# Projecting the queries of all eight heads in one pass of 512 columns, in place of two passes of 256

## The chip, the cores and the metric

One NeuronCore of a Trainium2 chip. The metric is the device time of one execution in microseconds. The profile's engines are PE (TensorE, the matmuls), DVE (VectorE), ACT (ScalarE), POOL (GpSimd) and SP (SyncE, which issues most DMAs).

## The reference

Two trunk layers over 512 latent tokens and 256 context tokens of width 1024. In each layer one input projection feeds three mixers: centred pooling, gated linear attention (GLA) and softmax attention with eight query heads and two key/value heads of 64 channels. The part of the softmax attention:

```python
u = (rmsnorm(x, g_mix) * (1 + sc1) + sh1) @ w_in        # and the same for the context, uc
p, gq, gk, gv, gg, rf, rb, aq, ak, av = split_in(u)     # aq: 512 columns, ak, av: 128 each
q = rmsnorm(q.reshape(B, N, 8, 64), g_q)                # per head, with a scale of 1/8 in the scores
ql = axial_rope(ql, rows, cols)                         # latent queries and keys only
o = softmax(q @ k.T / 8) @ v                            # latent queries see context and latent keys
mix = concat(pool_mixer(p), gla_output(o_gl, gg), o) @ w_out
x = x + ga1 * mix
x = x + ga2 * squared_relu_mlp(rmsnorm(x, g_mlp) * (1 + sc2) + sh2)
```

## The kernel before

Everything is fp32. For the large products each operand is split into a high and a low part in a rounded fp32 format (`whi`, `wlo` of the weights, `hTh`, `hTl` of the transposed activations), and each product is made of three matmuls: high by high, low by high, high by low. `tm_matmul` writes 128 tokens by some columns of weights: over 8 slices of the contraction it issues 24 matmuls for one token tile. Six token tiles are live in layer 0 (four latent, two context) and four in layer 1. `wcols` loads weights in pieces of 512 KB (`raw`, on SP's queue), ScalarE rounds them to `whi`, VectorE or GpSimd subtracts to `wlo`.

`q_proj(cb)` projects the queries of four heads: 256 columns for each live tile, one PSUM tile `tm` each, and ScalarE copies it to `Uq[cb][g]`, which holds up to three token tiles. After each group of three tiles (or the last tile) come `head_norm` (ScalarE squares into `sq`, VectorE sums it to `ssa`, makes the inverse root `rsa` in tiny steps, and multiplies, L874) and the rotary product `rope_mult`: four multiplications on GpSimd from `Uq` into `sq` (L863), one on VectorE in place (L865), which must wait until GpSimd has read `Uq`, and a sum (L866). The context queries in a group are multiplied by a gain instead. `q_proj(0)` goes over all tiles, then `q_proj(1)`.

The same stage holds GLA for two pairs of heads. For a pair, eight levels (s = 0, 1, 2, 4, ... 64) each make 48 or 24 small matmuls (`att`, L764) from `QQ` and `KK` (below s = 32 from a copy `kc` of `KK` that ScalarE makes). Between two levels VectorE multiplies `QQ` and `KK` in place by decays (L721, four per level), so the next level's matmuls wait for it. After the last level the chunks of `KK` are transposed (`kbt`), copied (`kbT`) and multiplied (`inc`). The output of a pair is `o`, then `ss`, `rg` and `ogl`, which ScalarE, VectorE, GpSimd and ScalarE (`mixh`) finish in turn.

What runs when is written as generators: `g` the GLA of both pairs, `a` the projections (`a_thread`: gates, keys and values, queries, and the pooling projections `p_proj`, whose PSUM tile is `fm`), `m` the modulation (`pm`, `pt`, `brow`), `t` the attention (`kT`, `qT`, `sc`, ...). A string of letters per layer deals out their steps; the first `t` runs what is left of `a`. A scheduler then fixes one order for each engine, and each engine runs its own in order:

```python
ths = {"g": gla_thread(), "a": at_, "m": mods, "t": att_}
for ch in STEPS[l]:
    if ch == "t":
        run(at_)
    next(ths[ch], None)
```

Of the kernel before, what the change touches and what calls it, by code (L numbers as in the profile page):

```python
# [14 lines left out]
ALU = mybir.AluOpType  # L15
# [6 lines left out]
KT = 8  # L22
# [12 lines left out]
def hybrid_kernel(ctx, tc, x, c, cx, c_ctx, w_mod, b_mod, g_mix, w_in, w_pool, s_pool, w_gate, b_gate,  # L35
# [20 lines left out]
    def slot(s, dt=F32, w=NT):  # L56
        return sp.tile([128, w], dt, tag="S", name=nm(s))
# [105 lines left out]
    def wcols(w, c0, n, ksplit, *more, sl=False):  # L163

        parts = []
        step = KT // ksplit
        for s in range(ksplit):
            parts.append(wload(*(w[s * step * 128:(s + 1) * step * 128, a:a + m].rearrange("(k p) n -> p k n", p=128)
                                 for a, m in ((c0, n),) + more), sl=sl))
        return lambda k: (parts[k // step][0][:, k % step], parts[k // step][1][:, k % step])  # L170
# [156 lines left out]
    def tm_matmul(ps, t, wk, hT, nk, c0=0, n=None, k0=0, k1=None):  # L327

        for k in range(k0, k1 or nk):
            wh, wl = wk(k)  # L330
            hh, hl = hT[k]
            sl = slice(t * 128, (t + 1) * 128)
            for i, (a, b) in enumerate(((hh, wh), (hl, wh), (hh, wl))):
                bb = b if n is None else b[:, c0:c0 + n]
                T.matmul(ps, a[:, sl], bb, start=(k == 0 and i == 0), stop=(k == nk - 1 and i == 2))  # L335
# [83 lines left out]
    for l in range(2):  # L419
# [163 lines left out]
        def gslot(s, tag, dt=F32, bufs=1, w=NT):  # L583
            return gp.tile([128, w], dt, tag=tag, name=nm(s), bufs=bufs)
# [52 lines left out]
        def gate_proj(pr):  # L637

            wk = wcols(W, C_GG + pr * 128, 128, 1)
            ps = psA("fm")  # L640
            fm_matmul(ps, wk, hT, KT, True, both)
            g_ = slot("gate")
            gx, tmp = g_[:, 0:N_], gslot("sg", "gt", bufs=GT)[:, 0:N_]
            A.activation(gx, ps[:, 0:N_], AF.Copy)
            gate[pr] = g_
            yield
            V.tensor_scalar(tmp, gx, -87.0, None, ALU.max)
            A.activation(tmp, tmp, AF.Exp, scale=-1.0)
            A.activation(tmp, tmp, AF.Ln, bias=one)
            A.activation(tmp, tmp, AF.Exp, scale=-1.0)  # L650
            V.scalar_tensor_tensor(gx, tmp, gglaT, gx, ALU.mult, ALU.mult)
# [205 lines left out]
        def rope_mult(v, tab, tmp, nt, nh):  # L857

            for half in range(2):
                for z in range(2):  # L860
                    d0 = half * 32 + z * 16
                    s0 = half * 32 + (1 - z) * 16
                    G.tensor_tensor(tmp[:, :, :, d0:d0 + 16], v[:, :, :, s0:s0 + 16],  # L863
                                    tab[:, 1, :, d0:d0 + 16].unsqueeze(2).to_broadcast([128, nt, nh, 16]), ALU.mult)
            V.tensor_tensor(v, v, tab[:, 0].unsqueeze(2).to_broadcast([128, nt, nh, 64]), ALU.mult)  # L865
            V.tensor_tensor(v, v, tmp, ALU.add)  # L866

        def head_norm(v, sq, nh, post=None):

            A.activation(sq, v, AF.Square)  # L870
            ss = mp.tile([128, nh], F32, tag="ssa", name=nm("ssa"))
            V.tensor_reduce(ss, sq, AX.X, ALU.add)
            r = rstd_of(ss, 64, "rsa", post)
            V.tensor_tensor(v, v, r.unsqueeze(2).to_broadcast([128, nh, 64]), ALU.mult)  # L874

        def k_proj():
            wk = wcols(W, C_AQ + 512, 256, 2)
            UK = slot("UK")
            UKt.append(UK)
            UV = slot("UV")  # L880
            UVt.append(UV)
            for t in alltiles:
                ps = psB("tm")
                tm_matmul(ps[:, 0:256], t, wk, hT, KT)
                A.activation(UK[:, t * 128:(t + 1) * 128], ps[:, 0:128], AF.Copy)
                A.activation(UV[:, t * 128:(t + 1) * 128], ps[:, 128:256], AF.Copy)  # L886
                yield
            sq = gslot("sq", "gt", bufs=GT)
            head_norm(UK.rearrange("p (m e) -> p m e", e=64), sq.rearrange("p (m e) -> p m e", e=64), 12)
            yield  # L890
            rope_mult(UK[:, 0:NL].rearrange("p (t h e) -> p t h e", h=2, e=64), rk,
                      sq[:, 0:NL].rearrange("p (t h e) -> p t h e", h=2, e=64), 4, 2)
            kc = UK[:, NL:NT].rearrange("p (m e) -> p m e", e=64)
            V.tensor_tensor(kc, kc, gr[:, 1].unsqueeze(1).to_broadcast([128, 4, 64]), ALU.mult)
            yield

        def q_proj(cb):
            wk = wcols(W, C_AQ + cb * 256, 256, 2)
            for t in live:
                g = t // 3  # L900
                if t % 3 == 0:
                    Uq[cb][g] = slot("Uq")
                uq = Uq[cb][g]
                ps = psB("tm")
                tm_matmul(ps[:, 0:256], t, wk, hT, KT)
                A.activation(uq[:, (t % 3) * 256:(t % 3) * 256 + 256], ps[:, 0:256], AF.Copy)
                yield
                if t % 3 == 2 or t == live[-1]:
                    nt = t % 3 + 1
                    sq = gslot("sq", "gt", bufs=GT)[:, 0:nt * 256]  # L910
                    uv_ = uq[:, 0:nt * 256]
                    head_norm(uv_.rearrange("p (m e) -> p m e", e=64), sq.rearrange("p (m e) -> p m e", e=64), nt * 4, 0.125)
                    yield
                    nr = nt if g == 0 else 1
                    u4 = uv_.rearrange("p (t h e) -> p t h e", h=4, e=64)
                    s4 = sq.rearrange("p (t h e) -> p t h e", h=4, e=64)
                    rope_mult(u4[:, 0:nr], rq[:, :, 3 * g:3 * g + nr], s4[:, 0:nr], nr, 4)
                    if nr < nt:
                        qc = uq[:, nr * 256:nt * 256].rearrange("p (m e) -> p m e", e=64)
                        V.tensor_tensor(qc, qc, gr[:, 0].unsqueeze(1).to_broadcast([128, (nt - nr) * 4, 64]), ALU.mult)  # L920
                    yield

        def p_proj(bp_):
            wk = wcols(W, bp_ * 128, 128, 1)
            ps = psA("fm")
            fm_matmul(ps, wk, hT, KT, True, both)
            m_ = slot("pm")
            A.activation(m_[:, 0:N_], ps[:, 0:N_], AF.Copy)
            pmt[bp_] = m_
            yield  # L930

        def a_thread():
            for qk in range(2):
                qk_proj(1, qk)
                yield
            for th in (gate_proj(0), gate_proj(1), k_proj(), q_proj(0), q_proj(1), p_proj(0), p_proj(1)):
                yield from th


# [384 lines left out]
```

## Time and profile before

| | us |
|---|---|
| median of three runs | 1680.46 (1678.68 to 1682.53) |
| the profiled execution | 1677.11 |
| its span | 1675.3 |
| TensorE busy | 1599.7 (95%) |
| VectorE busy | 910.4 (54%) |
| ScalarE busy | 642.4 (38%) |
| GpSimd busy | 414.2 (25%) |

The span runs from the first to the last instruction on the core; 1.8 us of the execution lie around it. A table of stretches gives, for each window of time, its length and the busy time of PE, weight loads (PEld), DVE, ACT and POOL, then the clock that TensorE was granted (1.00 is full speed), the busy share of the DMA engines and GB/s. In the group rows the last parts are busy time and mean ns of one, then the engine's idle time just before and what ended it. In the chain, each row is start, length and what the end of the program hung on at that time.

### The profile page before, as it was taken

The numbers are of one execution on the slowest core, as the hardware profiler recorded it, in microseconds if no ns is written. First come the engines' busy times: TensorE is split into PE (matmuls) and PEld (weight loads), VectorE is DVE, ScalarE is ACT, GpSimd is POOL, SyncE is SP. The second block draws the span as 40 slices with busy tenths as digits, with TensorE's granted clock in tenths as the row PEclk, the third lists the DMA queues.
The fourth block names the chain that finished last, engine by engine and source line by source line (L and its number), as shares of the span: only waits on it lengthen the run. The fifth ranks groups of instructions, "written<-read, shape, count | busy, mean of one in ns | idle before, by whom it ended". The sixth has DMA issues, their size and how long they took to land.

```text
span 1675.3 us, 27451 instructions
## 1 busy us (share of the span) xinstructions
PE 1599.7 (95%) x11403; PEld 1301.5 (78%) x11403; DVE 910.4 (54%) x1306; ACT 642.4 (38%) x1098; POOL 414.2 (25%) x484
## 2 busy tenths in 40 slices
PE   7999979999999999999999999897999999999997
PEld 4888856668888888888888889785667888888885
DVE  4437665743673654636546563586753645455544
ACT  5544445661531312213213244556662523223332
POOL 1121311212303032130321462241201122222225
PEclk9999989999999999999999999998999999999998
DMA  9445400222340421514424332100123313333331
GB/s 318 139 131 172 154 2 1 103 88 64 101 139 26 144 95 57 176 59 161 144 71 170 112 106 74 39 2 2 52 83 94 109 55 101 101 101 101 101 101 51
DMA packets 136636, 163.31 MB, mean 97 GB/s; under 512 B 9908, under 2 KB 108608, under 8 KB 136512
## 3 DMA queue, kind: packets, MB, share of 16 engines
q1 hardware_dynamic: 130176, 148.41, 27.7%
q10 hardware_dynamic: 5824, 13.12, 2.1%
q8 instruction: 89, 1.46, 0.4%
q14 instruction: 35, 0.29, 0.1%
q0 software_dynamic: 512, 0.03, 0.0%
HBM read 157.31 MB, written 4.23 MB: 96 GB/s over the span
## 4 chain that ended last, share of the span: by engine, by line
PE 85%; DVE 5%; ACT 4%; issue 2%; POOL 2%; DMA 2%; ACTq 0%; SPq 0%; POOLq 0%; DVEq 0%
PE dn L335 25%; PE up L316 19%; PE tm L335 7%; PE op L335 6%; PE up L318 5%; PE fm L316 4%; PE av L1055 3%; PE pT L1046 3%; PE up L325 2%; PE fm L318 1%; PE sc L1028 1%; PE att L764 1%; PE sc L1029 1%; PE pm L190 1%; DVE nmx L1031 1%
## 5 line engine op out<-in xcount | busy, mean ns | idle before, releaser
L159 ACT ACTIVATE whi<-raw 128x1024 fp32r<-128x1024 f32 (+2 forms) x182 | 185.0, 1031 | 568.6 <-PE dn L335 292.7
L1179 POOL TENSOR_TENSOR X<-X,rtmp 128x512 f32<-128x512 f32 x158 | 216.8, 1375 | 636.2 <-DVE rtmp L1178 636.0
L78 DVE TENSOR_TENSOR wlo<-raw,whi 128x1024 fp32r<-128x1024 f32 (+2 forms) x182 | 224.9, 1245 | 219.7 <-ACT whi L159 215.4
L1178 DVE TENSOR_TENSOR rtmp<-dn,ga 128x512 f32<-128x512 f32 x160 | 109.4, 688 | 213.4 <-PE dn L335 210.5
L335 PE MATMUL dn<-whi,ah 128*128 128x512 f32 x480 | 187.3, 390 | 0.0
L335 PE MATMUL dn<-whi,al 128*128 128x512 f32 x480 | 187.2, 390 | 0.0
L335 PE MATMUL dn<-wlo,ah 128*128 128x512 f32 x480 | 186.3, 390 | 0.0
L316 PE MATMUL up<-h2h,whi 128*128 128x512 f32 x464 | 182.5, 393 | 1.5 <-ACT relu L1221 1.5
L316 PE MATMUL up<-h2h,wlo 128*128 128x512 f32 x464 | 183.1, 395 | 0.0
L316 PE MATMUL up<-h2l,whi 128*128 128x512 f32 x464 | 182.8, 394 | 0.0
L335 PEld LDWEIGHTS dn<-whi,ah 128*128 128x128 f32 x480 | 90.1, 188 | 20.2 <-issue 0.8
L316 PEld LDWEIGHTS up<-h2h,whi 128*128 128x128 f32 x464 | 87.1, 188 | 23.4 <-ACT relu L1221 1.7
L335 PEld LDWEIGHTS dn<-whi,al 128*128 128x128 f32 x480 | 90.1, 188 | 19.5
L335 PEld LDWEIGHTS dn<-wlo,ah 128*128 128x128 f32 x480 | 90.1, 188 | 19.0
L316 PEld LDWEIGHTS up<-h2l,whi 128*128 128x128 f32 x464 | 87.1, 188 | 21.7 <-issue 2.5
L335 PE MATMUL tm<-whi,hTh 128*128 128x256 f32 (+1 forms) x352 | 102.2, 292 | 1.0 <-ACT UV L886 1.0
L316 PEld LDWEIGHTS up<-h2h,wlo 128*128 128x128 f32 x464 | 87.1, 188 | 19.5
L335 PE MATMUL tm<-whi,hTl 128*128 128x256 f32 (+1 forms) x352 | 100.7, 287 | 0.0
L335 PE MATMUL tm<-wlo,hTh 128*128 128x256 f32 (+1 forms) x352 | 100.3, 288 | 0.0
L335 PE MATMUL dn<-whi,a 128*128 128x512 f32 x320 | 99.9, 395 | 0.4 <-DVE rtmp L1178 0.4
L228 DVE SCALAR_TENSOR_TENSOR macc<-rawm,sstat,macc 128x1024 f32<-128x1024 f32 x56 | 75.6, 1370 | 7.9 <-DMA rawm<-in_w_mod_dram 7.4
L1031 DVE TENSOR_REDUCE nmx<-sc 128x1 f32<-128x768 f32 x64 | 60.6, 955 | 28.1 <-PE sc L1029 27.6
(295 smaller groups left out, 3329.9 us busy)
## 6 DMA issues: line engine op xcount, KB each, us to landing
rawm<-in_w_mod_dram SPq DMA_DIRECT2D x80, 512.0 KB, 5.6
raw<-in_w_up_dram SPq DMA_DIRECT2D x64, 512.0 KB, 4.2
raw<-in_w_down_dram SPq DMA_DIRECT2D x64, 512.0 KB, 4.4
raw<-in_w_in_dram SPq DMA_DIRECT2D x26, 512.0 KB, 4.0
rawm<-in_w_mod_dram SPq DMA_DIRECT2D x32, 256.0 KB, 5.4
raw<-in_w_out_dram SPq DMA_DIRECT2D x16, 512.0 KB, 4.4
raw<-in_w_in_dram SPq DMA_DIRECT2D x12, 256.0 KB, 3.0
ga<-gaD ACTq DMA_DIRECT2D x6, 512.0 KB
```

What stands on the lines that cost most here:

```text
L78: V.tensor_tensor(lo, full, hi.bitcast(F32), ALU.subtract)
L159: A.activation(hi, raw, AF.Copy)
L228: V.scalar_tensor_tensor(acc[s], raw, c_, acc[s], ALU.mult, ALU.add)
L316: T.matmul(ps[:, 0:NL], a, b[:, 0:NL], start=st, stop=sp_)
L318: T.matmul(ps[:, NL:NT], a, b[:, NL:NT], start=st, stop=sp_)
L325: T.matmul(ps[:, cs], a, b[:, cs], start=(k == 0 and i == 0), stop=(k == nk - 1 and i == 2))
L335: T.matmul(ps, a[:, sl], bb, start=(k == 0 and i == 0), stop=(k == nk - 1 and i == 2))
L1031: V.tensor_reduce(nmx[:, i:i + 1], sv, AX.X, ALU.max, negate=True)
L1046: T.transpose(pt_[:, i * 128:(i + 1) * 128], p_[:, ki * 128:(ki + 1) * 128], ident)
L1055: T.matmul(av_[64 * hh:64 * hh + 64, 0:256], vst, pe[:, hh * 256:hh * 256 + 256], start=(ki == 0), stop=(ki == len(kts) - 1))
L1178: V.tensor_tensor(tmp, ps, ga[0 if t < 4 else 1][:, sl], ALU.mult)
L1179: (V if b == NB - 1 and not both and t == 3 else G).tensor_tensor(X[t][:, sl], X[t][:, sl], tmp, ALU.add)
```

## The change

`q_proj` takes all 512 columns at once. For each live tile there are 24 matmuls of 512 columns in place of twice 24 of 256, in one PSUM tile, from which ScalarE copies two halves. The weights come in four pieces of 512 KB, of which all must be there for each tile, in place of two and two. The head norms and rotary products of the two halves follow each other after each group of tiles. In all 480 matmuls of 256 columns (and 480 weight loads) become 240 of 512; the counts of the other engines' instructions hardly change. A projection step now holds a tile of 512 columns, and the projection thread has 14 steps left of it where it had 20 in layer 0 and 12 where it had 16 in layer 1; the string that deals out the steps is the same.

```diff
-        def q_proj(cb):
-            wk = wcols(W, C_AQ + cb * 256, 256, 2)
+        def q_proj():
+            wk = wcols(W, C_AQ, 512, 4)
             for t in live:
                 g = t // 3
                 if t % 3 == 0:
-                    Uq[cb][g] = slot("Uq")
-                uq = Uq[cb][g]
+                    for cb in range(2):
+                        Uq[cb][g] = slot("Uq")
                 ps = psB("tm")
-                tm_matmul(ps[:, 0:256], t, wk, hT, KT)
-                A.activation(uq[:, (t % 3) * 256:(t % 3) * 256 + 256], ps[:, 0:256], AF.Copy)
+                tm_matmul(ps, t, wk, hT, KT)
+                for cb in range(2):
+                    A.activation(Uq[cb][g][:, (t % 3) * 256:(t % 3) * 256 + 256], ps[:, cb * 256:(cb + 1) * 256], AF.Copy)
                 yield
                 if t % 3 == 2 or t == live[-1]:
                     nt = t % 3 + 1
-                    sq = gslot("sq", "gt", bufs=GT)[:, 0:nt * 256]
...
+                    for cb in range(2):
+                        uq = Uq[cb][g]
+                        sq = gslot("sq", "gt", bufs=GT)[:, 0:nt * 256]
...
-            for th in (gate_proj(0), gate_proj(1), k_proj(), q_proj(0), q_proj(1), p_proj(0), p_proj(1)):
+            for th in (gate_proj(0), gate_proj(1), k_proj(), q_proj(), p_proj(0), p_proj(1)):
```

The orders differ in layer 0 from the first query tile to the first score, and in the same part of layer 1. In the rows below a name's number tells one buffer from another: `QQ_1163` and `KK_773` belong to GLA's first pair of heads, `QQ_2463` (before `QQ_2452`) and `KK_992` to its second, `Uq_1632`, `Uq_1644` and `Uq_1645` hold queries of the first three tiles, `UK` keys.

TensorE's queue in layer 0 at the level s = 64 of the first pair (`att` of 64x64), before; the `tm` rows are matmuls of one 256-column tile:

```order
L335 MATMUL tm_2041<-whi_1628,hTl_136 128x256
L764 MATMUL att_1957<-QQ_1163,KK_773 64x64 x2
L335 MATMUL tm_2041<-wlo_1629,hTh_135 128x256
L335 MATMUL tm_2041<-whi_1628,hTh_137 128x256
L764 MATMUL att_1957<-QQ_1163,KK_773 64x64 x22
L202 MATMUL pt_2030<-ident,brow_2024 128x128 x4
L335 MATMUL tm_2041<-whi_1628,hTl_138 128x256
```

and after, where the row on top ends a 512-column tile:

```order
L335 MATMUL tm_2026<-wlo_1641,hTh_141 128x512
L764 MATMUL att_1885<-QQ_1163,KK_773 32x32 x48
L190 MATMUL pm_995<-rawm_1999,sstat 32x512 x2
L190 MATMUL pm_995<-rawm_2003,sstat 32x512 x2
L764 MATMUL att_1960<-QQ_1163,KK_773 64x64 x24
L202 MATMUL pt_2013<-ident,brow_2007 128x128 x4
L695 MATMUL kbt_2054<-ident,KK_773 128x128 x6
L695 MATMUL kbt_2142<-ident,KK_773 128x128 x6
L190 MATMUL pm_2023<-rawm_2106,sstat 32x512 x2
```

The levels s = 32 and s = 64 and the transposes `kbt` now stand together, with only modulation matmuls between them; before, a good part of a tile stood ahead of each.

VectorE's queue at the same place, before (the rows on `tree` multiply `QQ` and `KK` for the next level, 12x32 behind s = 32 and 6x64 behind s = 64):

```order
L874 TENSOR_TENSOR Uq_1632<-Uq_1632,rsa_1845 128x768
L721 TENSOR_TENSOR QQ_1163<-QQ_1163,tree_1065 128x12x32
L721 TENSOR_TENSOR KK_773<-KK_773,tree_1065 128x12x32
L721 TENSOR_TENSOR QQ_1163<-QQ_1163,tree_1155 128x12x32
L721 TENSOR_TENSOR KK_773<-KK_773,tree_1155 128x12x32
L865 TENSOR_TENSOR Uq_1632<-Uq_1632,rq_756 128x768
L199 TENSOR_TENSOR brow_2024<-pm_995,brow_2024 128x512
L866 TENSOR_TENSOR Uq_1632<-Uq_1632,sq_1841 128x768
L78 TENSOR_TENSOR wlo_2157<-raw_2154,whi_2156 128x1024
L721 TENSOR_TENSOR QQ_1163<-QQ_1163,tree_1065 128x6x64
L721 TENSOR_TENSOR KK_773<-KK_773,tree_1065 128x6x64
L721 TENSOR_TENSOR QQ_1163<-QQ_1163,tree_1155 128x6x64
```

and after:

```order
L874 TENSOR_TENSOR Uq_1644<-Uq_1644,rsa_1861 128x768
L874 TENSOR_TENSOR Uq_1645<-Uq_1645,rsa_1950 128x768
L865 TENSOR_TENSOR Uq_1644<-Uq_1644,rq_756 128x768
L721 TENSOR_TENSOR QQ_1163<-QQ_1163,tree_1065 128x12x32
L721 TENSOR_TENSOR KK_773<-KK_773,tree_1065 128x12x32
L721 TENSOR_TENSOR QQ_1163<-QQ_1163,tree_1155 128x12x32
L721 TENSOR_TENSOR KK_773<-KK_773,tree_1155 128x12x32
L866 TENSOR_TENSOR Uq_1644<-Uq_1644,sq_1857 128x768
L199 TENSOR_TENSOR brow_2007<-pm_995,brow_2007 128x512
L865 TENSOR_TENSOR Uq_1645<-Uq_1645,rq_756 128x768
L721 TENSOR_TENSOR QQ_1163<-QQ_1163,tree_1065 128x6x64
L721 TENSOR_TENSOR KK_773<-KK_773,tree_1065 128x6x64
```

The norms of both halves and the first rotary product now stand ahead of the first four multiplications, and the second rotary product ahead of the last four.

TensorE's queue in layer 0 at `rg` of the first pair's output, before; `tm_2463` is the last query tile, and behind its 24 matmuls come the rest of the level `att_2570` and both `p_proj`:

```order
L190 MATMUL pm_2040<-rawm_2455,sstat 32x512 x2
L190 MATMUL pm_2040<-rawm_2459,sstat 32x512 x2
L764 MATMUL att_2503<-gq_935,KK_992 32x32 x48
L190 MATMUL pm_2040<-rawm_2555,sstat 32x512 x2
L190 MATMUL pm_2040<-rawm_2559,sstat 32x512 x2
L764 MATMUL att_2570<-QQ_2452,KK_992 32x32 x11
L828 MATMUL rg_2429<-ident,rsg_2420 64x128 x8
L828 MATMUL rg_2440<-ident,rsg_2420 64x128 x4
L335 MATMUL tm_2463<-whi_2150,hTh_127 128x256
L335 MATMUL tm_2463<-whi_2150,hTl_128 128x256
```

and after, where the row on top is the last of the second `p_proj`:

```order
L318 MATMUL fm_2367<-hTh_141,wlo_2364 128x256
L828 MATMUL rg_2440<-ident,rsg_2431 64x128 x8
L828 MATMUL rg_2451<-ident,rsg_2431 64x128 x4
L764 MATMUL att_2474<-gq_935,KK_992 32x32 x48
L764 MATMUL att_2534<-QQ_2463,KK_992 32x32 x48
L202 MATMUL pt_2668<-ident,brow_2662 128x128 x4
L1086 MATMUL qT_2697<-ident,Uq_1644 128x128 x3
L1086 MATMUL qT_2697<-ident,Uq_2024 128x128
L1086 MATMUL qT_2698<-ident,Uq_2024 128x128 x2
L1086 MATMUL qT_2998<-ident,Uq_1644 128x128 x3
L1086 MATMUL qT_2998<-ident,Uq_2024 128x128
L764 MATMUL att_2597<-QQ_2463,kc_2598 32x32 x48
```

Both `p_proj` and the last query tiles have moved ahead of `rg`, and the first levels of the second pair, the key and query transposes and the first scores follow it directly.

More of the change, by code (lines that the diff above doesn't have):

```diff
@@ L909, in q_proj @@
                     nt = t % 3 + 1
-                    sq = gslot("sq", "gt", bufs=GT)[:, 0:nt * 256]
[L911 to L921, printed above, removed]
+                    for cb in range(2):
+                        uq = Uq[cb][g]
+                        sq = gslot("sq", "gt", bufs=GT)[:, 0:nt * 256]
+                        uv_ = uq[:, 0:nt * 256]
+                        head_norm(uv_.rearrange("p (m e) -> p m e", e=64), sq.rearrange("p (m e) -> p m e", e=64), nt * 4,
+                                  0.125)
+                        yield
+                        nr = nt if g == 0 else 1
+                        u4 = uv_.rearrange("p (t h e) -> p t h e", h=4, e=64)
+                        s4 = sq.rearrange("p (t h e) -> p t h e", h=4, e=64)
+                        rope_mult(u4[:, 0:nr], rq[:, :, 3 * g:3 * g + nr], s4[:, 0:nr], nr, 4)
+                        if nr < nt:
+                            qc = uq[:, nr * 256:nt * 256].rearrange("p (m e) -> p m e", e=64)
+                            V.tensor_tensor(qc, qc, gr[:, 0].unsqueeze(1).to_broadcast([128, (nt - nr) * 4, 64]), ALU.mult)
+                        yield
         def p_proj(bp_):
```

## The prediction

> **What bounds the kernel now.** I read the page first, for the engine that sets the end, then a table of stretches, for where that engine idles, then groups, waits and the chain inside the stretches that the change touches.
>
> ```profile
> span 1675.3 us, 27451 instructions
> PE 1599.7 (95%) x11403; PEld 1301.5 (78%) x11403; DVE 910.4 (54%) x1306; ACT 642.4 (38%) x1098; POOL 414.2 (25%) x484
> PE 85%; DVE 5%; ACT 4%; issue 2%; POOL 2%; DMA 2%; ACTq 0%; SPq 0%; POOLq 0%; DVEq 0%
> raw<-in_w_in_dram SPq DMA_DIRECT2D x26, 512.0 KB, 4.0
> ```
>
> TensorE is busy 95% of the span and is 85% of the chain that ends last. So two things can move the time: the length of the matmul stream, and the few stretches where TensorE waits. The stretches around the query projection, first of layer 0, then (from 1134) of layer 1; the granted clock stands after POOL's busy time:
>
> ```profile
> 130.00:140.00 10.00, 9.58 (x254) 9.18 (x253) 5.83 (x15) 4.10 (x10) 0.00 (x0) 1.00 0.66 225
> 140.00:150.00 10.00, 8.79 (x156) 6.57 (x156) 7.53 (x16) 2.59 (x5) 2.71 (x4) 1.00 0.35 118
> 150.00:160.00 10.00, 10.00 (x255) 8.51 (x254) 8.19 (x17) 7.35 (x22) 2.56 (x4) 1.00 0.22 57
> 160.00:170.00 10.00, 9.91 (x148) 7.47 (x147) 8.53 (x22) 5.52 (x11) 2.49 (x6) 1.00 0.85 274
> 220.00:230.00 10.00, 6.86 (x227) 4.95 (x225) 7.64 (x17) 5.70 (x10) 2.80 (x5) 0.98 0.02 5
> 230.00:240.00 10.00, 7.34 (x194) 5.71 (x194) 8.83 (x16) 3.65 (x7) 2.71 (x8) 0.51 0.01 2
> 250.00:260.00 10.00, 10.00 (x112) 7.06 (x112) 5.45 (x10) 6.25 (x13) 0.00 (x0) 0.82 0.01 2
> 1134.00:1140.00 6.00, 1.84 (x71) 1.40 (x70) 1.59 (x3) 3.13 (x6) 2.68 (x3) 0.80 0.01 3
> ```
>
> From 150 to 170 TensorE is full although VectorE works 8.2 and 8.5 of 10 us: the 256-column query tiles stand between the gated-linear-attention (GLA) levels and hide the chains that those levels need. Where that cover ends (220 to 240, 1134 to 1140) TensorE starves and the granted clock drops to about a half: 0.51 follows a stretch with 3.14 us of idle time.
>
> **The matmuls themselves.** 480 matmuls of 256 columns become 240 of 512. Their prices in the chain:
>
> ```profile
> 129.96 3.60 PE tm L335 x30
> 175.22 5.95 PE tm L335 x48
> 168.98 3.07 PE tm L335 x24
> 513.27 32.66 PE dn L335 x144
> ```
>
> One of 256 columns costs 5.95/48 = 124 ns, or at its best 3.60/30 = 120.0 ns; one of 512 costs 32.66/144 = 226.8 ns. A pair of 256 gives 248 or 240, so a 512 saves 21 or 13 ns, and 240 of them 5.0 or 3.1 us. I take 4.0 and keep both ends. The Trainium skill, "TensorE: Matmul & The Clock Gate", section "Wait — 56ns, not 53.3ns?", says that warm matmuls start N/2.4 GHz plus about 2.5 ns apart; by it a pair saves only 2.5 ns, an estimate of 0.6 us in all, which would put my time some 3.4 us higher. The rows show five to eight times that per pair, and the measured rows decide.
>
> The weights are the same bytes in four pieces of 512 KB, as before, but all four must now be there for the first tile: two pieces come earlier. They are asked for on SP's queue behind modulation loads, and a piece lands in 4.0 us. In the rows of 130 to 150, where the tiles stand, the DMA engines are at 0.66 and 0.35, so there is room, and the last piece is first used some three quarters into the first tile. I cost this at nothing; if that cover were gone, one landing of 4.0 us would stand in the first tile.
>
> **The order: levels of the first pair of heads.** The program's steps are dealt out by a fixed string; a projection step is now twice as long, there are six fewer of them in layer 0 and four fewer in layer 1, and so all later steps meet other work. Behind the third tile TensorE runs one level's matmuls, one whole tile, the level s = 32, and then nothing but the level s = 64, a modulation transpose (pt) and the chunk transposes (kbt). Before, most of a tile stood ahead of each. On VectorE the normalisations (L874) of both halves and the first rotary product (L865), which waits for POOL, stand ahead of the four multiplications (L721) that the level s = 64 needs; the second rotary product stands ahead of the four that kbt needs. Prices, from 140 to 170 (VectorE) and 140 to 235 us:
>
> ```profile
> L874 DVE TENSOR_TENSOR Uq<-Uq,rsa 128x768 f32<-128x768 f32 x2 | 1.9, 954 | 0.0
> L872 DVE TENSOR_REDUCE ssa<-sq 128x12 f32<-128x768 f32 x2 | 1.9, 953 | 1.6 <-ACT sq L870 1.6
> L784 DVE COPY_PREDICATED dg<-mask,att 128x192 f32<-128x192 int32 x6 | 1.9, 365 | 0.0
> L865 DVE TENSOR_TENSOR Uq<-Uq,rq 128x768 f32<-128x768 f32 x1 | 0.9, 946 | 0.0
> L199 DVE TENSOR_TENSOR brow<-pm,brow 128x512 f32<-128x512 f32 x1 | 0.7, 677 | 0.0
> L260 DVE SCALAR_TENSOR_TENSOR rsa<-rsa,ssa 128x12 f32<-128x12 f32 x2 | 0.3, 172 | 0.2
> L863 POOL TENSOR_TENSOR sq<-Uq,rq 128x192 f32<-128x192 f32 x8 | 4.8, 633 | 14.2 <-DVE Uq L874 14.2
> L906 ACT ACTIVATE Uq<-tm 128x256 f32<-128x256 f32 x11 | 4.2, 384 | 22.9 <-PE tm L335 22.8
> L870 ACT ACTIVATE sq<-Uq 128x768 f32<-128x768 f32 x4 | 3.4, 840 | 0.2
> 162.94 0.47 DVE QQ L721
> 152.39 3.18 PE tm L335 x25
> 156.06 0.91 PE att L764 x62
> 164.96 0.85 PE kbt L695 x6
> 165.81 1.85 PE pm L190 x16
> ```
>
> Count from the end of the third tile. ScalarE: two evictions (0.77) and two squares (1.68), first square done at 1.6, second at 2.4. VectorE: two reductions to 3.5; two multiplications and two predicated copies of the level (0.5 and 0.37 each) to 5.3; ten tiny steps of some 0.2 (0.17 and the gap) to 7.3; the two L874 to 8.3 and 9.2. POOL's first set of four (2.5) ends at 10.8, L865 at 11.8, four L721 at 13.7. TensorE: level 1.0, modulation 0.9, a tile of 24 x 227 ns = 5.4, level 1.0, modulation 0.5 or so: free at 8.9. It waits 4.8 us. Then the level s = 64 (0.5) ends at 14.2; pt waits for the other half of the rotation (0.95) and L199 (0.68) until 15.3, 1.1 us; kbt waits for the second L865 and two L721 until 17.2, with pt at 0.6 another 1.3 us. Together 7 us where TensorE before waited 0.09 (160 to 170). Of the 1.6 us that it waited from 130 to 150 some may go, since fewer and larger steps run there. I take +5.5; bounds +2 (POOL's set hidden in another order of arrivals) and +8.
>
> The half clock comes with such a wait. In the row of 250 to 260 TensorE is full at 0.82, so 1.8 us are lost while it has work; the second loss (0.51) fell where it mostly waited. I take +1.7; bounds 0 and 3.5. The same page, section "HAM oscillation — how this bites in real kernels", says that only gaps over about 3.4 us bring the half clock; by it a wait cut into pieces of 1 to 3 us costs nothing and this term is 0. The row of 230 to 240, at 0.51 behind 3.14 us of idle time in pieces, speaks against it: the longest is the 2.3 us of qT, in the waits below.
>
> **The order: ahead of attention in layer 0.** Both pooling projections (p_proj, 48 matmuls each) and the last query tile stood behind the GLA output and between the first levels of the second pair. They now stand ahead of it, and from rg to the first score only levels and transposes are left.
>
> ```profile
> 196.93 1.53 PE rg L828 x24
> 222.63 0.82 PE kT L985 x6
> 229.67 0.77 PE L1028 MATMUL sc<-kh,qs 128*128 128x512 f32 x1 [0.84 <-DVE dg L784]
> PE qT L1081 <- DVE qs L78: 2.3, 1, 2.3
> L745 ACT ACTIVATE kc<-KK 128x768 f32<-128x768 f32 x5 | 4.4, 871 | 3.9 <-DVE KK L721 3.9
> L834 POOL TENSOR_TENSOR ogl<-ogl,gate 128x768 f32<-128x768 f32 x1 | 1.8, 1836 | 5.7 <-PE tm L335 5.7
> L836 ACT ACTIVATE mixh<-ogl 128x768 fp32r<-128x768 f32 x1 | 0.8, 846 | 0.0
> ```
>
> Before, kT to the first score took 229.67 - 222.63 = 7.0 us, 3.1 of them idle (2.3 and 0.8). Now, from the end of rg: ScalarE copies ogl (1.0), VectorE multiplies (to 2.1), POOL gates it (1.84, to 4.0), ScalarE rounds it (0.85, to 4.8) and only then makes the first kc (0.87, to 5.7), behind which the third level, kT, kh, kl and the next kc stand in line with some eight L721 (4 us) on VectorE between them. By that line the first score comes 12 to 15.6 us after rg, of which TensorE has work for 6.7 (four levels at 0.91, kT, and at kT's 0.14 each sixteen transposes): 5 to 9 us idle instead of 3.1. I take +4.5 of the difference 2 to 6, since the clock is then half as in the row of 230 to 240; bounds 0 (the attention that follows starves on VectorE anyhow, and these multiplications are out of its way) and +8.
>
> **Layer 1** loses the cover in the same way: of the four tiles one is left behind the levels, and both p_proj come ahead of the output (o, ss, rg).
>
> ```profile
> PE kT L985 <- ACT pm L928: 2.9, 1, 2.9
> PE sc L1028 <- ACT dg L780: 2.3, 1, 2.3
> 193.62 0.99 PE pm L190 x8
> ```
>
> New waits by rows: the way from ss to rg, which in layer 0 lasts from 193.62 to 196.93 = 3.3 us, was covered by p_proj and now has 0.7 us of level work: 2.6; the chunk transposes behind the last level, some 1 for the multiplications and 2 for ScalarE's copies behind two squares of 0.84. Against this kT no longer waits 2.9 for an eviction of p_proj, but the same gate and rounding then hold the first score. I take +2; bounds -3 and +6.
>
> **Sum** for the profiled execution: 1675.3 span and 1.8 around it, 1677.1. -4.0 + 5.5 + 1.7 + 4.5 + 2 = +9.7. It ran 3.4 us below the median of the three runs shown (1680.46); on that median the time is **1690**.
>
> **The rivals.**
> *Faster.* POOL decides: had its first rotary set ended by the time TensorE is through the s = 32 level, that is 4 us earlier than I count, the L721 would be early and the levels covered; p_proj ahead of the output would likewise let VectorE finish the second pair's start early. For it speaks that VectorE has 1.5 us of slack per 10 from 150 to 170; against it that L865 waits for POOL in a queue without choice. Only the saving is left: 1680.5 - 4 = 1676.5. Chance 0.15.
> *No change.* The wait ahead of attention is repaid, since VectorE is the bound there from 220 to 240 (7.64, 8.83) and has less left to do, and layer 1 comes out even: -4 + 5.5 = +1.5, 1682. Chance 0.16.
> *Much slower.* The half clock stays through kbt, inc and the next tile, and returns ahead of attention, each time for ten us as in the row of 230 to 240, where 7.34 us of TensorE time at half the clock are 3.7 lost: 7.3 in place of 1.7, so 1696. Chance 0.13.
> *The rows of 512 are no cheaper here* than two of 256, since these share the stream with small level matmuls: 1690 + 4 = 1694. Chance 0.05.
> The forecast itself, 1685 to 1694, has 0.51.
>
> **The numbers.** A change under 0.2% (3.4 us) can't be told from none. Slower: 0.51 + 0.13 + 0.05 = 0.69; same 0.16; faster 0.15. The range leaves out most of the faster case and the end of the much slower one: 1678 to 1702.
>
> **What would show it.** In the changed kernel's trace: query tiles of 24 matmuls in 5.4 to 5.5 us; a TensorE wait of 3 to 5 us on VectorE's L721 behind the s = 32 level, near 163 us, with the rotary set's end ahead of it, and a granted clock near a half within the next 10 us; 5 to 9 us idle between rg and the first score in layer 0; waits of 1 to 3 us ahead of kbt, inc and rg in layer 1. I am wrong if TensorE is full from 150 to 170 as before, or if the time lost ahead of attention comes back within it.

## The result, and the profile after

The changed kernel takes 1695.34 us (median of four runs, 1694.07 to 1696.82), the kernel before 1679.92 on the same chip (1678.68 to 1682.53): ratio 1.0090, interval 1.0076 to 1.0103, or 15.4 us more. The forecast was 1690 (1678 to 1702), 9.7 us more. The profiled execution took 1696.2 us. One execution of a kernel in the experiments (the changed one without the rotary product) took 1809.58 us at a granted clock of 0.84 where the others of it had 0.98 or more; it is left out of that kernel's median.

The top of its page:

```profile
span 1694.4 us, 26961 instructions
PE 1604.8 (95%) x11163; PEld 1293.5 (76%) x11163; DVE 911.5 (54%) x1306; ACT 641.1 (38%) x1098; POOL 414.7 (24%) x484
```

TensorE lost 240 matmuls and is busy 5 us longer than before (1599.7). The table of stretches (length, busy PE, weight loads, VectorE, ScalarE, GpSimd, then the granted clock) shows where:

```profile
140.00:150.00 10.00, 10.00 (x163) 7.04 (x168) 6.97 (x15) 2.91 (x6) 2.40 (x4) 1.00 0.14 42
160.00:170.00 10.00, 7.24 (x130) 5.04 (x128) 7.86 (x21) 5.91 (x19) 6.34 (x8) 1.00 0.52 163
170.00:180.00 10.00, 8.74 (x94) 6.59 (x95) 7.05 (x17) 3.34 (x6) 2.17 (x4) 0.66 0.35 98
210.00:220.00 10.00, 10.00 (x73) 7.42 (x66) 3.01 (x8) 1.33 (x3) 2.84 (x6) 1.00 0.01 2
230.00:240.00 10.00, 3.41 (x107) 2.53 (x107) 9.78 (x22) 7.31 (x13) 0.84 (x2) 0.76 0.01 2
240.00:250.00 10.00, 5.96 (x173) 4.86 (x174) 9.75 (x17) 3.53 (x7) 2.70 (x8) 0.56 0.01 2
1150.00:1160.00 10.00, 5.21 (x98) 4.17 (x96) 4.39 (x11) 4.19 (x10) 3.23 (x3) 0.67 0.01 2
1160.00:1170.00 10.00, 7.69 (x89) 5.97 (x89) 8.11 (x10) 6.25 (x11) 2.81 (x9) 0.65 0.00 0
```

From 160 to 180, where TensorE was full before (9.91 and 10.00 of 10 us), it now waits 4.0 us and runs at 0.66 of its clock behind the wait. From 230 to 240 it has 3.4 us of work, and VectorE is the engine that is full. The two layers' stages, each from its first level matmul to the first matmul of the output projection, before:

```profile
115.97:366.59 250.62, 231.91 (x3095) 172.26 (x3091) 159.36 (x298) 139.70 (x308) 56.89 (x97) 0.97 0.24 83
1057.08:1254.98 197.90, 177.16 (x2172) 134.75 (x2171) 137.35 (x263) 121.79 (x257) 47.63 (x77) 0.97 0.10 34
```

and after:

```profile
117.71:375.99 258.28, 231.74 (x2950) 166.33 (x2946) 162.12 (x298) 139.09 (x308) 60.40 (x97) 0.94 0.24 79
1067.57:1274.60 207.03, 179.52 (x2076) 131.56 (x2075) 135.64 (x262) 119.97 (x256) 44.98 (x77) 0.95 0.10 32
```

Layer 0's stage is 7.7 us longer and layer 1's 9.1. In layer 0 the idle time (length less TensorE's busy time) grows by 7.8 us, from 18.7 to 26.5; in layer 1 by 6.8, from 20.7 to 27.5, and the busy time by 2.4 although the matmuls are shorter, with the clock lower (0.95 against 0.97). These are two single executions, which lie 19.1 us apart (1677.11 and 1696.2), more than the medians (15.4); so the 16.8 us of the two stages are somewhat too many. The waits of TensorE that are new or longer, in layer 0 from 95 to 260 us:

```profile
PE qT L1086 <- DVE qs L78: 4.0, 1, 4.0
PE att L764 <- DVE dg L784: 3.6, 2, 2.0
PE att L764 <- DVE KK L721: 3.6, 3, 2.3
PE kbt L695 <- ACT AT L777: 0.8, 1, 0.8
```

and all of 1 us and more in layer 1 from 1094 to 1165:

```profile
PE sc L1033 <- ACT kh L998: 5.6, 2, 4.1
PE fm L316 <- ACT z L669: 2.7, 1, 2.7
PE inc L703 <- ACT kbT L696: 1.1, 1, 1.1
PE kbt L695 <- ACT sq L870: 1.1, 1, 1.1
PE kbt L695 <- ACT AT L777: 1.0, 1, 1.0
```

### The profile page after: what moved, and what is told of

The parts are those of the page before. It is cut to its first block, busy times and chain, and to the rows that moved or that the text cites. A ratio compares the mean times of both kernels' runs of the same rounds, so it can differ in the third digit from the quotient of the medians.

```text
span 1694.4 us, 26961 instructions
## 1 busy us (share of the span) xinstructions
PE 1604.8 (95%) x11163; PEld 1293.5 (76%) x11163; DVE 911.5 (54%) x1306; ACT 641.1 (38%) x1098; POOL 414.7 (24%) x484
## 4 chain that ended last, share of the span: by engine, by line
PE 84%; DVE 6%; ACT 3%; DMA 2%; POOL 2%; issue 2%; SPq 0%; ACTq 0%; POOLq 0%; DVEq 0%
PE dn L335 25%; PE up L316 19%; PE tm L335 7%; PE op L335 6%; PE up L318 5%; PE fm L316 4%; PE av L1060 3%; PE pT L1051 3%; PE up L325 2%; PE fm L318 1%; PE sc L1033 1%; PE sc L1034 1%; PE att L764 1%; DVE nmx L1036 1%; PE pm L190 1%
## 5 line engine op out<-in xcount | busy, mean ns | idle before, releaser
L335 PEld LDWEIGHTS dn<-whi,ah 128*128 128x128 f32 x480 | 90.2, 188 | 20.2 <-DVE rtmp L1183 0.8
L335 PE MATMUL tm<-whi,hTh 128*128 128x288 f32 (+2 forms) x272 | 87.4, 323 | 1.0 <-ACT UV L886 1.0
L335 PE MATMUL tm<-whi,hTl 128*128 128x288 f32 (+2 forms) x272 | 86.7, 320 | 0.0
L335 PE MATMUL tm<-wlo,hTh 128*128 128x288 f32 (+2 forms) x272 | 86.3, 321 | 0.1
```

## The experiments

Where a ratio is given, it is against the kernel before on the same chip; the change itself has 1.0090.

**Which layer.** Two kernels make the change in one layer only.

```diff
-for th in (..., k_proj(), q_proj(), p_proj(0), p_proj(1)):
+qs_ = (q_proj(),) if l == 0 else (q_half(0), q_half(1))     # and l == 1 in the other
+for th in (..., k_proj(), *qs_, p_proj(0), p_proj(1)):     # q_half: q_proj of the kernel before
```

> Layer 0 projects its queries in one pass of 512 columns, layer 1 in two passes of 256 as before. Theory (waits in both layers): layer 0's part of the loss, which the two traces put at 7.9 us (the delay between the same instructions of the two traces grows from 1.5 to 9.4 us there), so about 1688 us against 1680 before. Rival (the loss is mostly layer 1's or lies elsewhere): within 3 us of before. Rival (the layers' waits share a cause such as the weights' arrival): the full 1695.

> Layer 1 in one pass of 512, layer 0 in two of 256. Theory: layer 1's part, 7.4 us by the same comparison, so about 1687 us; my prediction had put this layer at +0.4 (2 us of waits less 1.6 of saving), which would give 1680 to 1681. The two single-layer runs should add up to the whole (+15.4) if the layers are independent.

Layer 0 alone: 1686.39 us, 1.0031 (1.0020 to 1.0042), some 5 us. Layer 1 alone: 1686.54 us, 1.0037 (1.0021 to 1.0054), some 6 us. Both layers lose, and together they give 0.68% of the 0.90; the missing 0.22% is just within what the intervals allow. Layer 1's share is not the 0.4 us that I had counted.

**The matmul itself.** The same steps, evictions and norms, with each tile as two passes of 256 columns in one PSUM tile.

```diff
-tm_matmul(ps, t, wk, hT, KT)
+for cb in range(2):
+    tm_matmul(ps[:, cb * 256:cb * 256 + 256], t, wk, hT, KT, cb * 256, 256)
```

> The changed program with every tile's 24 matmuls of 512 columns written as two passes of 24 matmuls of 256 columns into the same PSUM tile; steps, weights, evictions, norms and rotary products as in the change. The order that comes out puts parts of a tile ahead of the levels s = 32 and 64 in layer 0 again. Theory (the waits come from the steps, the wider matmul saves some 4 us): the saving is lost (+4) and the wait of 4 us behind s = 32 goes (-4 to -5.7 with its half clock), about 1694 to 1696. Rival (512 columns themselves cost the time, by slower streaming): back near 1680 to 1684.

1702.20 us, 1.0126 (1.0108 to 1.0144): slower than the change by some 6 us, and above the numbers of the theory and of the rival. That the 512 columns themselves cost the time is not borne out. The order came out differently too, so the run does not price the wider matmul alone. The expected gain behind s = 32 did not show in the time: the chunk transposes kbt now waited 2.3 us for VectorE, and ahead of attention one level waited 5.7 us for kh.

**The rotary product.** The changed kernel and the kernel before, each without the rotary product of the queries.

```diff
-rope_mult(u4[:, 0:nr], rq[:, :, 3 * g:3 * g + nr], s4[:, 0:nr], nr, 4)
```

> The changed kernel without the rotary product of the queries (GpSimd's four multiplications and VectorE's product and sum are left out; the keys keep theirs). TensorE's order stays that of the change. Theory (GpSimd's two sets back to back hold VectorE's queue, and with it the level multiplications, in layer 0 behind s = 32 and in layer 1 ahead of the second pooling projection): the waits of 2.3 + 0.9 + 0.8 us in layer 0 fall below 1 us together, the 2.7 us in layer 1 goes; with the half clock that follows, about 8 us less than the change: 1687. Rival (the bare levels wait for their own chain anyway, GpSimd is not in it): 1692 or more.

> The kernel before with the same work left out. Theory: its rotary products were mostly under cover; the chain of layer 1 shows GpSimd's set, but TensorE then still works on pooling projections: 1677 to 1680. The difference to the run beside it then falls from 15.4 to 7 to 10 us. Rival: it falls as much as the changed kernel does, the difference stays 15.

Without it the changed kernel takes 1689.24 us (median of five), 1.0055 (1.0042 to 1.0069), and the kernel before 1680.25, 1.0003 (0.9992 to 1.0014). Before, the product was free; after the change some 6 us of the 15 go with it (0.9% falls to 0.5% between the two); 1689.2 lies between the theory's 1687 and the rival's 1692. With GpSimd's multiplications VectorE's product and sum are gone as well, so the run does not tell the wait for GpSimd from VectorE's own work. The first run's waits from 150 to 180 us, the longest ahead of attention, and the two stages:

```profile
PE kbt L695 <- DVE KK L721: 0.6, 1, 0.6
PE att L764 <- DVE KK L721: 0.5, 1, 0.5
PE att L764 <- ACT kh L995: 5.7, 1, 5.7
```

```profile
116.01:375.52 259.51, 232.83 (x2950) 165.57 (x2946) 154.35 (x290) 139.35 (x308) 49.78 (x81) 0.94 0.24 79
1066.25:1269.49 203.24, 179.48 (x2077) 131.89 (x2076) 128.69 (x254) 119.81 (x256) 35.27 (x61) 0.95 0.10 33
```

The 4.0 us behind s = 32 shrink to 1.1 (and 0.5 for a transfer) and layer 1's 2.7 us are gone, as the theory has it. But only layer 1's stage is shorter (by 3.8 us); layer 0's is not (259.5 against 258.3): there the time came back ahead of attention, where one level now waited 5.7 us for kh.

**The rotary product in a tile of its own**, so that VectorE's product need not wait until GpSimd has read the queries.

```diff
-V.tensor_tensor(v, v, tab[:, 0]..., ALU.mult)
-V.tensor_tensor(v, v, tmp, ALU.add)
+V.tensor_tensor(rot, v, tab[:, 0]..., ALU.mult)
+V.tensor_tensor(v, rot, tmp, ALU.add)
```

> The changed kernel, with VectorE's rotary product written to a tile of its own: it no longer waits until GpSimd has read the queries; the sum behind it does. This moves the wait by one instruction and lets the order put part of a tile ahead of s = 64 and the norm of the second half behind the level. Theory: 3 to 5 us better than the change (1690 to 1692), since the sum still waits for GpSimd in the same queue. Rival (the wait in place is the whole of it): below 1688.

1703.02 us, 1.0138 (1.0121 to 1.0155): worse than the change. In layer 1 the second pooling projection now waited longer:

```profile
PE fm L316 <- ACT z L669: 6.3, 1, 6.3
```

Both guesses fell: to move the wait by one instruction within the same queue took nothing away. Which part of the new order made it worse was not followed up.

**The pooling projections back in their place**, by empty steps ahead of them.

```diff
+def idle():
+    for _ in live:
+        yield
-for th in (..., q_proj(), p_proj(0), p_proj(1)):
+for th in (..., q_proj(), idle(), p_proj(0), p_proj(1)):
```

> The changed kernel with as many empty steps between the query and the pooling projections as the change took away in tiles (six in layer 0, four in layer 1), so that both pooling projections come again behind the GLA output and between the second pair's levels. The levels s = 32 and 64 of the first pair stay bare. Theory: the waits ahead of attention (9.3 us from rg to the first score in layer 0 against 3.1 before) and layer 1's 2.7 us ahead of the second pooling projection and part of its 4.1 us ahead of the first score go; the 4 us behind s = 32 stay: 1686 to 1688. Rival (the bare levels and the half clock behind them are the main cost): 1692 or more.

1701.78 us, 1.0124 (1.0106 to 1.0143), 20.7 us above the 1681.03 beside it: the theory's number is missed by far, and on the other side. The rival's (1692 or more) holds, but the largest wait is not the rival's. In layer 1 the output product o now stood without cover and waited:

```profile
PE o L807 <- DVE st L712: 5.8, 1, 5.8
```

In layer 0 the idle time fell to 23.9 us, but the stage took 260.8, since TensorE's busy time rose to 236.9 (231.7 in the change); the clock over the stage was 0.94 in both. Where part of such a rise comes from is shown below, at the steps of before.

My reading, which no further run tried: the pooling projections had covered one chain in the kernel before; in this order they cover another, and a third is bare.

**The queries ahead of the keys**, so that the keys' six tiles stand behind the queries' norms.

```diff
-k_proj(), q_proj(), p_proj(0), p_proj(1)
+q_proj(), k_proj(), p_proj(0), p_proj(1)
```

> The changed kernel with the query projection ahead of the key and value projection, whose six tiles of 256 columns then stand behind the queries' norms. Theory (what costs is that both halves' norms and rotary products fall due where little TensorE work is left before the levels end): the sets end under the key tiles, the 2.7 us in layer 1 and most of layer 0's 4 us go, and the keys' one set comes late instead: 1685 to 1690. Rival (any order of the same steps leaves the levels of the second pair bare ahead of attention, and this is the main cost): 1693 to 1697.

1693.89 us, 1.0080 (1.0061 to 1.0098), the same as the change within the intervals; the rival's number. The waits behind layer 0's levels fell from 4.0 us to 0.8 and the 2.7 us in layer 1 to 0.7, as the theory had it, but in layer 1 a level waited 4.7 us for VectorE and kbt 2.4, and in layer 0 a modulation matmul waited 2.1 us for its weights.

**The gating of the first pair's output later**, with TensorE's order as in the change; and the same in the kernel before.

```diff
+if li == 6 and fin:          # in levels(), ahead of s = 32; fin holds the three lines below of pair 0
+    fin.pop()()
...
-G.tensor_tensor(ogl..., gate...); A.activation(hi..., ogl...); G.tensor_tensor(lo..., ogl..., hi...)
+fin.append(finish)
```

> The changed kernel, with the last part of the first pair's GLA output (GpSimd's gating, ScalarE's rounding to mixh, GpSimd's low part) issued behind the second pair's level s = 32 instead of right behind rg. TensorE's order stays that of the change; ScalarE no longer waits for GpSimd ahead of the first copies kc and, in layer 1, ahead of kh. Theory (this wait is part of the bare way from rg to the first score): layer 0's way of 15.3 us from the end of rg shortens by 1.5 to 3 us, layer 1's wait of 4.1 us ahead of the first score by 2 to 3; together 3 to 6 us better than the change: 1690 to 1692. Rival (that way is held by VectorE's level multiplications and roundings alone, GpSimd is beside it): 1694 to 1697.

> The kernel before with the same late gating as in the run of the changed kernel beside it. Theory (the gating hurts only where nothing covers it): layer 0 unchanged, layer 1's wait of 2.9 us ahead of the key transposes shrinks by 1 to 2 us: 1677 to 1680. Rival: as much better as the changed kernel, 1675 or less.

In the expectation the words are "behind" s = 32; the edit puts it ahead of the matmuls of that level, as the diff shows. But GpSimd's queue has nothing else at this place, and GpSimd runs its own queue: in layer 0 the gating ran right behind rg in the change (first row) and still did in this run (second row). What moved was ScalarE's rounding (from 227.0 to 235.4) and GpSimd's low part (from 227.9 to the third row):

```profile
225.15 1.81 POOL L834 TENSOR_TENSOR ogl<-ogl,gate 128x768 f32<-128x768 f32 x1 [9.86 <-DVE ogl L833]
224.19 1.81 POOL L841 TENSOR_TENSOR ogl<-ogl,gate 128x768 f32<-128x768 f32 x1 [9.85 <-DVE ogl L837]
236.41 1.82 POOL L843 TENSOR_TENSOR mixl<-ogl,mixh 128x768 fp32r<-128x768 f32 x1 [3.07 <-ACT mixh L842]
```

The changed kernel with it: 1693.04 us, 1.0088 (1.0074 to 1.0102), between the two numbers and not to be told from the change. Layer 0's stage is 257.5 against 258.3, and the way from the end of rg to the first score 14.3 us against 15.3. So the rounding and the low part held at most 1.0 us of that way; of the gating itself the run says nothing. In layer 1's stage the profile shows 202.2 against 207.0, and the first score waits 1.3 us instead of 4.1, but this is the fastest of its five executions (1688.85), and the timed runs do not bear out a gain of that size. The kernel before with it: 1676.32 us, 0.9986 (0.9975 to 0.9997), a gain of some 2 us, between theory and rival; its key transposes waited 0.2 us instead of 2.9. This is the only kernel here that beats both, by an interval that nearly reaches 1.

**The steps of before.** Each 512-column tile in two halves of the contraction, on the very steps where the 256-column tiles stood. There is one string per layer and one word per step: h stands for a tile and its half, n and r for the norm and the rotary set of a half of the heads and a group of tiles.

```diff
+QPLAN = ('h00 h01 h10 . . h11 h20 h21 n00 r00 h30 h31 h40 n10 r10 h41 h50 h51 n01+n11 r01+r11',
+         'h00 h01 h10 . . h11 n00 r00 h20 h21 h30 n10 r10 h31 n01+n11 r01+r11')
...
+tm_matmul(pst[t], t, wk, hT, KT, k0=h * 4, k1=h * 4 + 4)
```

> 512 columns, but each tile's matmuls in two halves of the contraction, dealt out on exactly the steps where the kernel before had its 256-column tiles; norms and rotary products at most where they stood before, the last two sets in the last two query steps; layer 1 with groups of two tiles. So TensorE's work per step is that of before, and both pooling projections stand where they stood. The order that comes out nevertheless uses the tiles up by the level s = 8 and leaves s = 16, 32 and 64 with modulation matmuls only. Theory (cover counts at the level that waits, not in the sum): layer 0's first levels lose 4 us or more again, the way to attention is like before, 1686 to 1692. Rival (the number of steps is what counts): 1676 to 1680, the saving alone.

1692.49 us, 1.0086 (1.0070 to 1.0102), at the upper end of the theory. So equal steps don't restore the time. Layer 0's stage and two of its stretches (the traced execution took 1697.1, 4.6 above the median):

```profile
117.43:377.57 260.14, 239.46 (x2951) 167.22 (x2947) 162.03 (x298) 139.26 (x308) 59.89 (x97) 0.94 0.24 79
160.00:170.00 10.00, 6.44 (x163) 3.56 (x160) 8.80 (x23) 7.26 (x22) 5.05 (x8) 0.80 0.40 134
170.00:180.00 10.00, 10.00 (x76) 6.73 (x75) 4.93 (x13) 1.62 (x2) 0.00 (x0) 0.86 0.50 159
```

TensorE idles 20.7 us in this stage, only 2 more than before, and yet the stage is as long as the change's: its busy time is 239.5 us against 231.9 before and 231.7 in the change. The waits behind s = 16 to 64 are short, none over 1.0 us, but they lie close together, and the clock falls behind them. That is the smaller part of the 7.7 us: the stage's clock is 0.94 here and in the change. The larger part stands in the 116 modulation matmuls (pm), which take 16.2 us in the change's stage (first row: its length, their time on PE, their weight loads) and 21.9 here, some of them at the half clock:

```profile
117.71:375.99 258.28, 16.20 (x116) 3.15 (x112) 0.94 0.24 79
117.43:377.57 260.14, 21.89 (x116) 3.31 (x112) 0.94 0.24 79
```

In this order they stand in smaller groups between other work, and a group of four took as long as one of eight; first eight in the change, then four here:

```profile
165.84 1.06 PE L190 MATMUL pm<-rawm,sstat 128*32 128x512 f32 x8
173.71 1.05 PE L193 MATMUL pm<-rawm,sstat 128*32 128x512 f32 x4
```

**Layer 0 in an order that keeps a tile ahead of each level**, layer 1 as before, the late gating in both.

```diff
+QPLAN = ('h00 h01 h10 h11 h20 h21 h30 h31 n00 r00 h40 h41 n10 r10 h50 h51 n01 r01 n11 r11', '')
...
+pst[t] = psA("tm")[:, 0:512]        # psB in the run above; psA: the two buffers that the levels use
```

> 512 columns in layer 0 alone, layer 1 as before, the late gating in both. In layer 0 each tile is dealt out in two halves of the contraction on two steps, a fourth tile comes ahead of the first norm, one half's norm and rotary set falls due per pair of steps, and the tile's PSUM buffer is taken from the two that the levels use, so that a tile can no longer run ahead of the levels that it should cover: in TensorE's order a whole tile then stands between s = 8, 16 and 32, most of one between the parts of s = 64, and on VectorE the level multiplications stand ahead of both halves' norms. Both pooling projections stand behind rg as before. Theory (layer 0's 5 to 8 us were the order, the matmuls save 0.4 us per tile): 2 to 3 us less than the kernel before with late gating (1676.3), so 1673 to 1675. Rival (waits of a microsecond and the half clock behind them come back in any such order): 1679 to 1683.

1686.39 us, 1.0038 (1.0024 to 1.0052): some 9 us above the kernel before with late gating, and on the wrong side of the rival's numbers too. Layer 1's stage takes 196.0 us, no more than before, so the loss is all layer 0's: its stage takes 263.3, with 28.3 us of idle time and 20.2 us in the modulation matmuls. The longest wait of TensorE from 120 to 215 us:

```profile
PE pm L193 <- DMA rawm<-in_w_mod_dram: 5.1, 3, 2.9
```

It is a new one. Modulation weights (rawm) and split weights share buffers in the code (the tags hi and lo of one pool), and the four pieces of the query weights are all held until the last tile; that this is why the loads came late is read from the code and was not tried by itself.

## Why the prediction was right or wrong

*The matmuls (-4.0).* Right. In the chain after, two tiles in a row:

```profile
178.62 11.10 PE tm L335 x48
```

231 ns for 512 columns against 248 for two of 256, 17 ns, times 240 is 4.1 us. The rule for warm matmuls in the Trainium skill ("TensorE: Matmul & The Clock Gate", section "Wait — 56ns, not 53.3ns?"), by which a pair saves 2.5 ns, is not borne out by these rows.

*The levels of the first pair (+5.5).* The mechanism was right. The chain behind the third tile, which ended at 156.4:

```profile
162.16 0.88 DVE Uq L874
164.32 1.70 POOL sq L863 x3
166.04 1.34 DVE Uq L865
168.17 0.93 DVE KK L721
170.48 1.57 PE att L764 x44
```

L874, GpSimd's set, L865, the multiplications, then the level s = 64: as counted. The size was too large: 2.3 + 0.9 us of waits for this level instead of 4.8, no wait of pt instead of 1.1, and 0.8 ahead of kbt instead of 1.3, for ScalarE's copies (AT) and not for the second L865; 4.0 in all instead of 7. VectorE's chain was not shorter: the multiplications ended 14.0 us after the tile, where I had 13.7. It got through the tiny steps of both halves in 1.0 us where I had 2.0, but then ran slower beside GpSimd, whose two sets lasted from 163.2 to 169.5: L865 took 1.34 us and three multiplications 0.93 or 0.94, against 0.94 and 0.54 just behind it. What made the wait smaller is TensorE, which was free 1.6 us later than counted. The 1.6 us that TensorE waited from 130 to 150 before are gone, so the net is 2.4. And without this wait (the run with no rotary product) layer 0 was not shorter: time won here is waited for ahead of attention.

*The half clock (+1.7).* The mechanism was right, the size too small. In the row of 170 to 180 a third of the clock is missing from 8.74 us of work: 3.0 us. It is one piece at half speed:

```profile
171.00:177.00 6.00, 5.22 (x56) 4.18 (x52) 4.85 (x11) 2.85 (x6) 2.17 (x4) 0.50 0.12 25
```

Over layer 0's stage TensorE's busy time is the same as before, although six tiles are shorter by 2.5 us in all, which makes this term about 2.3. I had left out the row of 230 to 240 before as mostly waiting, but it has 7.34 us of work at 0.51. The rule in the Trainium skill ("TensorE: Matmul & The Clock Gate", section "HAM oscillation — how this bites in real kernels") names gaps over some 3.4 us; read as a threshold, as I read it, it does not hold here: a wait of 2.3 and one of 0.9 us brought 0.66, and in the run with the steps of before waits of at most 1.0 us brought 0.80 and 0.86.

*Ahead of attention in layer 0 (+4.5).* The size was right, the mechanism only in part. From the end of rg (223.7) to the first score (239.0) are 15.3 us, within the 12 to 15.6 counted; TensorE idles 8.3 of them instead of 3.1 before, so 5.2. The chain that ended last does not go through GpSimd's gating and mixh, which I had put first:

```profile
222.27 1.46 PE rg L828 x24
228.94 1.94 DVE KK L721 x2
235.38 1.03 DVE KK L721 x2
```

Behind the first two levels it is VectorE's queue, but for one copy by ScalarE (kc, 0.85 us). The line that I had counted was only just shorter: it came to the first kc at 228.83, and VectorE's mask copy, for which the third level waited, ended at 228.86. Nor is GpSimd out of the way: while its gating ran (225.15 to 226.96), a multiplication on VectorE took 1.80 us, and the next one 0.55:

```profile
225.57 1.80 DVE L721 TENSOR_TENSOR QQ<-QQ,z 128x384 f32<-128x384 f32 x1 [0.58 <-PE att L764]
227.30 0.55 DVE L721 TENSOR_TENSOR KK<-KK,z 128x384 f32<-128x384 f32 x1
```

Two more took 1.94 together beside GpSimd's low part, and 0.98 in the run that moved it. No run moved the gating itself. VectorE has 3.0 us of work from 210 to 220, under the pooling projection, and 9.78 and 9.75 from 230 to 250: its work for the second pair falls due after its idle time instead of within it.

*Layer 1 (+2 for waits, -1.6 of the saving).* This is the term that was most mis-sized. The stage grew by 9.1 us, by 10.7 with the saving taken out, in place of 2; the run with layer 1 alone measured some 6 net. Of the waits I named, kbt and inc came (1.0, 1.1 and 1.1 us), the one of 2.6 ahead of rg hardly (0.3 and 0.4). The set-off ahead of attention came too: the first two scores wait 5.6 us (4.1 and 1.5), and before the key transposes and the same scores waited 6.7, the 2.9 and 2.3 of the prediction and

```profile
PE sc L1028 <- ACT kh L993: 1.5, 1, 1.5
```

Two things were absent from the count. The second pooling projection waits 2.7 us for a chain that I did not follow, though both sets of GpSimd stand in it back to back as in layer 0:

```profile
1127.83 3.71 POOL sq L863 x4
1131.57 0.96 DVE Uq L865
1135.57 0.91 DVE z L673
1137.35 0.80 ACT z L669
1138.19 7.38 PE fm L316 x24
```

GpSimd's set holds L865, L865 holds VectorE's next work, that holds ScalarE's copy of z, and only then does fm start. The other is the half clock, which I costed at nothing here: these 24 matmuls take 7.4 us where the 24 of the first pooling projection, just ahead, took 5.6, the rows of 1150 to 1170 stand at 0.67 and 0.65, and the stage's busy time is 2.4 us longer in place of 1.6 shorter.

*The whole.* That the time fell into the range is in part luck. The terms of layer 0 make +9.3 (with its 2.4 of the saving), those of layer 1 +0.4; changed alone, the layers cost some 5 and 6 us. One was counted too high and the other far too low, and the sum, 9.7 against 15.4, hides it.

*The transfers, costed at nothing.* Right for the change, which shows no wait for weights in these stages; two of the other orders had one, of 2.1 and 5.1 us.

What stays open is whether an order exists in which the 4 us saved by the wider matmuls remain. The other orders tried here did not show one.

## What to carry to other kernels

A wider matmul saves on the engine that is the bound, but in a queue of fixed order the narrow tiles were also the cover of other engines' chains, and the norms of both halves fall due together: list for each wait what stands ahead of it before and after, in every layer that has the change. Count the clock with the waits: here 4.0 us of waits, in pieces of 0.8 to 2.3, cost another 3 in the work behind them. Look at the engine that becomes full in the bare stretch (here VectorE), and at what slows it, even where that is beside the chain. Whether it helps to make its work fall due while it is idle was not tried by itself. And an instruction that stands later in the program has not moved unless its engine's queue has something else to run ahead of it: look in the trace.

## What the runs showed of the hardware

The granted clock fell behind waits that were shorter than I had expected to matter: in the run with the steps of before, five waits of 0.3 to 1.0 us within 7 us were followed by stretches at 0.80 and 0.86. That stage had 7.7 us more of TensorE time than the change's 231.7, with less idle time (20.7 us against 26.5): 5.8 us of idle time were won back, and more than that went into TensorE's own work: 5.7 us into the modulation matmuls in their smaller groups, the rest into the clock and what was not followed up.

VectorE's multiplications of 128x384 (L721) took 0.93 or 0.94 us beside GpSimd's rotary sets of the first pair's levels, 1.80 beside its gating, and 0.54 or 0.55 just behind each.
